# Output projection: normalized rows transposed by VectorE squares and quarter transfers instead of by TensorE

## The chip, the cores and the metric

The kernel runs on one core of a Trainium2 chip. The metric is the device time of one execution in microseconds (us); a lower time is better. The engines are named as in the profile: PE is TensorE (PEld its weight loads), DVE is VectorE, ACT is ScalarE, POOL is GpSimd, SP is SyncE, which here only issues transfers. The sixteen DMA engines move what SP, ACT and POOL issue. SBUF has 128 partitions; "quarter" below means 32 of them.

## What is computed

One decoder layer on 2048 tokens of width 1024, in float32. Two mixers (gated linear attention and dilated window attention) give `mixed`; the part around the change is the output projection, the norm behind it and the first matrix of the MLP:

```python
mixed = jnp.concatenate([o_a, o_b], axis=-1).astype(h.dtype)
h = h + jnp.einsum('bsm,md->bsd', mixed, w_out[l])

nm = rmsnorm(h, mlp_norm_g[l])
a = jnp.square(jax.nn.relu(jnp.einsum('bsd,df->bsf', nm, w_ff1[l])))
h = h + jnp.einsum('bsf,fd->bsd', a, w_ff2[l])
...
return rmsnorm(h, final_norm_g)
```

`rmsnorm(x, g)` is `x * rsqrt(mean(x*x) + 1e-6) * g` along a row.

## The kernel before

Matrix products are made from fp32r parts: each operand is split in a high part (ACT, L543) and the rest (DVE, L544), and `mm3` (L140 to L142) adds three matmuls. The big products use a scheme with seven block products in place of eight, so sums and differences of blocks are needed on both sides. The order of work on each engine comes from a planner: it places the instructions of the program by a timeline that it works out itself, and gives out the 25 slots of a shared pool of tiles (`slot`, L127) on the way; on the chip, each engine then executes its list strictly in that order and waits where an operand isn't there. A few instructions are pinned to the order of the program.

The stage of the output projection starts at L1379. Tokens lie in 16 tiles of 128 rows, taken as eight pairs (`tiles`, L1444: tile i and i+4 of a half, four pairs in each half of the tokens). Pairs 0 and 1 are made by plain products (loop at L1656), pairs 2 to 7 by the seven-product scheme (`product0`, L1634, called 42 times by the loop at L1689, with `prep0` three products ahead and four buffers `mcomb`). `load_mix` and `load_x` bring the inputs of later pairs: x of pair p+1 is issued at the third product of pair p. `mix_block` (L1465) transposes the mixer's rows on PE; the change does not touch it.

When the rows of a tile are complete, `row_done` (L1622) stores them to `hD` and queues `norm_row` for them, and after the second tile of a pair `norm_sums` too; `next_norm` (L1629) takes one of these after the first, second and sixth product of a pair, and three more in the next stage (L1871).

- `norm_row(h, t)` squares the 128x1024 rows into `scr` with a sum (ACT, L1393), makes the reciprocal root (L174, L175), scales the rows in place (DVE, L1395), transposes them on PE in eight blocks of 128x128 into two PSUM banks "c" (L1400), and copies the banks to two quarters of `bb` (ACT, L1401): `hb4[0]`, `hb4[1]` for the first tile of a pair, `hb4[2]`, `hb4[3]` for the second. `store_T` (L1385) then stores what is an operand as it stands: two blocks of the first tile, one of the second.
- `norm_sums(t, x)` makes the four sums of blocks on DVE (L1408 to L1411), one in `bb`, three in the pair's `xh` tile, and stores them.

`scr` (the second half of the tile `gs`, L1379) and `bb` are single buffers for all rows; `xh` tiles come from the shared pool and go back to it when the sums in them are stored. The stores go to `hTD` in DRAM on SP's queue. The next stage reads `hTD` in pieces (L1425), splits them (`hb`) and multiplies them with `w_ff1`, which comes through the tiles `w1raw` (L1488, POOL's queue): half 0 of the tokens, pairs 0 to 3, towards the end of this stage (`token_pieces(0, ...)`, L1688), half 1 much later.

Of the kernel before, what the change touches and what calls it, by code (L numbers as in the profile page):

```python
# [13 lines left out]
AF = mybir.ActivationFunctionType  # L14
# [4 lines left out]
D = 1024  # L19
# [95 lines left out]
def emit(tc, a, stop=99):  # L115
    nc = tc.nc
    V, A, G, T, SP = nc.vector, nc.scalar, nc.gpsimd, nc.tensor, nc.sync
# [6 lines left out]
    def ps(tag):  # L124
        return psum.tile([128, 512], F32, name="ps_" + tag, tag=tag, bufs=BANKS[tag])

    def slot(name, dt=F32, n=SLOT):  # L127

        return up.tile([128, SLOT], dt, name=name, tag="u", bufs=25)[:, :n]

    def view(t, shape):
        n = int(np.prod(shape))
        names = "abcd"[:len(shape)]
        return t[:, :n].rearrange(f"p ({' '.join(names)}) -> p {' '.join(names)}", **dict(zip(names, shape)))
# [15 lines left out]
    ident = const.tile([128, 128], F32, name="ident")  # L150
# [14 lines left out]
    def stat(n=1):  # L165
        if stat_at[0] + n > 44:
            stat_at[0] = 0
        s = stats[:, stat_at[0]:stat_at[0] + n]
        stat_at[0] += n
        return s  # L170

    def rstd_of(ssq, width, n=1, bias=eps):
        r = stat(n)
        A.activation(r, ssq, AF.Ln, bias=bias, scale=1.0 / width)  # L174
        A.activation(r, r, AF.Exp, scale=-0.5)  # L175
        return r
# [369 lines left out]
    def x_load(t, dst):  # L546
        SP.dma_start(dst, x2[t * 128:t * 128 + 128])
# [13 lines left out]
    def transposed(xt, last=None, pin=False, by=ident):  # L561
        out = []
        for q in range(2):
            pv = view(ps("cd"[q]), (4, 128))
            for k in range(4):
                of = xt[:, (4 * q + k) * 128:(4 * q + k + 1) * 128]
                ins = T.transpose(pv[:, k, :], last if last is not None and 4 * q + k == 7 else of, by)
                if pin and q + k == 0:
                    tc.keep_in_program_order(ins)
            out.append(pv)  # L570
        return out
# [33 lines left out]
    def second_half():  # L605

        b = [view(bp[:, 512 * q:], (4, 128)) for q in range(4)]
        for i in range(4):
            for k in range(2):
                x_load(8 + 4 * k + i, xp[:, D * k:D * k + D])  # L610
            yield
            for k in range(2):
                xt = xp[:, D * k:D * k + D]
                ss = stat()
                tc.keep_in_program_order(A.activation(bp[:, :D], xt, AF.Square, accum_out=ss))
                r = rstd_of(ss, D)
                V.scalar_tensor_tensor(xt, xt, r, gB, op0=OP.mult, op1=OP.mult)
            yield
            for k in range(2):
                for q, pv in enumerate(transposed(xp[:, D * k:], pin=True, by=perm)):  # L620
                    A.activation(b[2 * k + q], pv, AF.Copy)
                yield
            (b11, b21, b12, b22), (t2, t4, t3) = b, [view(xp[:, 512 * q:], (4, 128)) for q in range(3)]
            V.tensor_tensor(b12, b12, b11, op=OP.subtract)
            V.tensor_tensor(t2, b22, b12, op=OP.subtract)
            for j, v in ((2, b21), (1, b11), (5, b12), (6, t2), (3, b22), (4, t4), (7, t3)):
                if j == 5:
                    yield
                    V.tensor_tensor(t4, b21, t2, op=OP.subtract)
                    V.tensor_tensor(t3, t2, b11, op=OP.subtract)  # L630
                SP.dma_start(nTD[j - 1][:, :, i * 128:i * 128 + 128], v)
            yield

    pairs, outs = {}, {}

# [33 lines left out]
    with tc.manual_schedule(engines={nc.tensor.engine, nc.vector.engine, nc.scalar.engine, nc.gpsimd.engine}):  # L669
# [29 lines left out]
        def turned(t):  # L699
            return transposed(xs[t], by=perm)  # L700
# [6 lines left out]
        pv = turned(0)  # L707
# [9 lines left out]
        pv = turned(1)  # L717
# [6 lines left out]
        pv = turned(2)  # L724
# [6 lines left out]
        pv = turned(3)  # L731
# [17 lines left out]
        pv = turned(4)  # L749
# [5 lines left out]
        pv = turned(5)  # L755
# [4 lines left out]
        pv = turned(6)  # L760
# [4 lines left out]
        pv = turned(7)  # L765
# [60 lines left out]

    of_wo = split_wo()
    other, back, bias = second_half(), [], bias_rows()
    for at in range(7, len(jobs)):
        g = jobs[at][0]  # L830
# [512 lines left out]
    for k in range(-AHEAD, NU + LAG):  # L1343
        tr, pv, sc = iter(()), iter(()), iter(())
        if 0 <= k < NU:
            tr = units[k].transpose()
        if 0 <= k - LAG:
            u = units[k - LAG]
            u.b.v = vs[u.b.h // 2, u.b.br]
            pv = u.values()  # L1350
# [28 lines left out]
    gs, bb = slot("gs"), slot("bb")  # L1379
    gM, scr = gs[:, :D], gs[:, D:2 * D]  # L1380
    hb4 = [view(bb[:, 512 * q:], (4, 128)) for q in range(4)]
# [3 lines left out]
    def store_T(t, *which):  # L1385
        half, i = t // HT, t % 4
        for j, q in which:
            SP.dma_start(hTD[half, j - 1][:, :, i * 128:i * 128 + 128], hb4[q] if isinstance(q, int) else q)

    def norm_row(h, t):  # L1390

        ss = stat()
        A.activation(scr, h, AF.Square, accum_out=ss)  # L1393
        r = rstd_of(ss, D)
        V.scalar_tensor_tensor(h, h, r, gM, op0=OP.mult, op1=OP.mult)  # L1395
        k = t % HT // 4
        for q in range(2):
            pv = view(ps("c"), (4, 128))
            for c in range(4):
                T.transpose(pv[:, c], h[:, (4 * q + c) * 128:(4 * q + c + 1) * 128], ident)  # L1400
            A.activation(hb4[2 * k + q], pv, AF.Copy)  # L1401
        store_T(t, *(((1, 0), (2, 1)) if k == 0 else ((3, 3),)))

    def norm_sums(t, x):

        b11, b21, b12, b22 = hb4
        t2, t4, t3 = [view(v, (4, 128)) for v in (x[:, 0, :512], x[:, 0, 512:], x[:, 1, :512])]
        V.tensor_tensor(b12, b12, b11, op=OP.subtract)  # L1408
        V.tensor_tensor(t2, b22, b12, op=OP.subtract)
        V.tensor_tensor(t4, b21, t2, op=OP.subtract)  # L1410
        V.tensor_tensor(t3, t2, b11, op=OP.subtract)  # L1411
        store_T(t, (5, b12), (6, t2), (4, t4), (7, t3))
# [209 lines left out]
    def row_done(p, e):  # L1622
        t = tiles[2 * p + e]
        SP.dma_start(hD[t * 128:t * 128 + 128], xhs[p][:, e])
        norms.append((norm_row, xhs[p][:, e], t))
        if e:
            norms.append((norm_sums, t, xhs[p]))
# [28 lines left out]
    for at in range(4):  # L1656
        p, e = divmod(at, 2)
# [31 lines left out]
    for g in range(14, 56):  # L1689
        p, i = divmod(g, 7)  # L1690
# [261 lines left out]
def build(nc, inputs, stop=99):  # L1952
    arrays, aps = {}, {}
    for name in _INS:
        arrays[name] = np.ascontiguousarray(inputs[name])
    arrays.update(_constants())
    for name, v in arrays.items():
        aps[name] = nc.dram_tensor(name, v.shape, mybir.dt.from_np(v.dtype), kind="ExternalInput").ap()
    aps["out"] = nc.dram_tensor("out", (1, S, D), F32, kind="ExternalOutput").ap()
    with tile.TileContext(nc, schedule_with_timeline_sim=True) as tc:  # L1960
        emit(tc, aps, stop)
    return arrays
# [10 lines left out]
```

## Time and profile before

| | us |
|---|---|
| median of three runs | 2228.05 |
| lowest and highest of the three | 2226.95, 2230.27 |
| span of the profiled execution, first to last instruction | 2224.1 |
| the rows are normalized (first L1393 to last L1401) | about 869.5 to 1057 |
| transfers issued by SP to `hTD`, L1388 | 56 of 256 KB |

The profiled execution's time is known as its span; what lies around the span is the 4 us by which the median exceeds it. Times of instructions are counted from the span's start. A row of a timeline gives the start, the duration, engine, line, operation, output and input tiles and how many are merged. A row of a group gives the smallest, median and largest duration in ns. "SPq" is the time in which SP's sequencer issues a transfer, not the transfer itself; "to landing" is from the issue until all of its data have arrived. In a row of waits stand the total in us, the number of waits and the longest.

### The profile page before, as it was taken

Reading aid. Unit: us, or ns where it says so; the run is one execution under the profiler, and the core shown is the slowest. Engines: PE = TensorE matmul, PEld = TensorE weight load, DVE = VectorE, ACT = ScalarE, POOL = GpSimd, SP = SyncE. Lnnn points to the kernel's source line nnn. Section 1 sums busy time; section 2 is a strip of 40 time slices with the busy share of each in tenths; the row PEclk is TensorE's granted clock in tenths of the full one; section 3 lists DMA queues with packets and bytes.
Section 4 is the critical chain, followed back from the end, with each engine's and each line's share of the span. In section 5 each row is a group of like instructions: output and inputs, shape, how many; then the busy total and the mean of one; then the engine's idle time right before and its main releaser. Section 6 shows DMA issues by size and latency. Waiting matters only on the chain.

```text
span 2224.1 us, 34980 instructions
## 1 busy us (share of the span) xinstructions
PE 2205.2 (99%) x12420; PEld 1914.9 (86%) x12420; DVE 1651.5 (74%) x3092; ACT 1238.8 (56%) x2422; POOL 590.1 (27%) x625
## 2 busy tenths in 40 slices
PE   9999999999999999999999999999999999999998
PEld 8988998899999998888788888888888888888887
DVE  8676766666777877769776788777776697576788
ACT  7365424536888884547555566555555433333446
POOL 1000000035578673000000000000008543042563
PEclk9999999999999999999999999999999999999999
DMA  6566866777977976868654466555489988687775
GB/s 210 177 215 190 265 186 187 240 248 257 314 241 224 291 260 231 269 220 264 198 151 142 139 181 195 151 182 154 130 286 288 308 293 269 216 265 236 272 258 187
DMA packets 322740, 499.89 MB, mean 225 GB/s; under 512 B 20808, under 2 KB 225243, under 8 KB 311301
## 3 DMA queue, kind: packets, MB, share of 16 engines
q1 hardware_dynamic: 284434, 340.02, 47.0%
q0 software_dynamic: 30784, 104.94, 16.7%
q10 hardware_dynamic: 7346, 52.70, 6.3%
q8 instruction: 98, 1.61, 0.3%
q14 instruction: 78, 0.63, 0.1%
HBM read 339.45 MB, written 162.85 MB: 226 GB/s over the span
## 4 chain that ended last, share of the span: by engine, by line
PE 74%; issue 14%; DMA 4%; DVE 4%; ACT 2%; POOL 1%; SPq 1%; POOLq 0%; DVEq 0%; ACTq 0%
PE ps_a L142 7%; PE ps_a L141 7%; PE ps_a L140 7%; PE ps_c L142 6%; PE ps_c L141 6%; PE ps_c L140 6%; PE ps_a L1001 4%; PE ps_d L140 4%; PE ps_d L141 4%; PE ps_d L142 4%; PE ps_o L140 3%; PE ps_o L142 3%; PE ps_o L141 3%; PE ps_d L982 2%; PE ps_c L964 2%
## 5 line engine op out<-in xcount | busy, mean ns | idle before, releaser
L543 ACT ACTIVATE cb<-bs 128x1024 fp32r<-128x1024 f32 x104 | 110.3, 1060 | 286.7 <-PE ps_o L141 104.9
L544 DVE TENSOR_TENSOR cb<-bs,cb 128x1024 fp32r<-128x1024 f32 x104 | 151.7, 1459 | 129.0 <-ACT cb L543 128.5
L1488 POOL DMA_DIRECT2D w1raw<-w_ff x64 | 48.0, 750 | 701.1 <-DVE mcomb L544 504.5
L544 DVE TENSOR_TENSOR mcomb<-w1raw,mcomb 128x512 fp32r<-128x512 f32 x224 | 154.2, 689 | 93.1 <-ACT mcomb L543 93.1
L1778 POOL TENSOR_TENSOR bs<-bs,rb 128x1024 f32<-128x1024 f32 x60 | 169.4, 2824 | 201.8 <-DMA bs<-w_ff 196.5
L543 ACT ACTIVATE mcomb<-w1raw 128x512 fp32r<-128x512 f32 x224 | 140.5, 627 | 79.8 <-PE ps_c L142 26.7
L1001 PE MATMUL ps_a<-v,pt 128*128 128x65 f32 x1200 | 177.3, 253 | 1.1 <-ACT pt L989 0.7
L1001 PEld LDWEIGHTS ps_a<-v,pt 128*128 128x128 f32 x1200 | 172.7, 194 | 2.9 <-ACT pt L989 1.3
L973 ACT ACTIVATE pe<-pe,O 128x256 f32<-128x256 f32 (+1 forms) x384 | 156.2, 453 | 13.1 <-DVE O L972 10.7
L982 PE MATMUL ps_d<-ident,pe 128*128 128x128 f32 x600 | 158.6, 280 | 1.1 <-ACT pe L973 1.1
L972 DVE CUSTOM_DVE_ANT_0 pe<-ps_c,nb 128x256 f32<-128x256 f32 (+1 forms) x384 | 126.6, 360 | 39.6 <-PE ps_d L982 20.8
L304 ACT ACTIVATE wcomb<-wraw 128x512 fp32r<-128x512 f32 (+2 forms) x119 | 90.3, 759 | 111.9 <-PE ps_a L141 52.6
L544 DVE TENSOR_TENSOR ca<-ra,ca 128x1024 fp32r<-128x1024 f32 x84 | 132.6, 1579 | 0.1
L140 PE MATMUL ps_c<-hb,mcomb 128*128 128x512 f32 x320 | 124.9, 390 | 0.3 <-ACT xs L1568 0.3
L141 PE MATMUL ps_c<-hb,mcomb 128*128 128x512 f32 x320 | 124.6, 389 | 0.0
L142 PE MATMUL ps_c<-hb,mcomb 128*128 128x512 f32 x320 | 124.3, 389 | 0.0
L142 PE MATMUL ps_c<-cb,ca 128*128 128x512 f32 x312 | 121.5, 389 | 0.0
L140 PE MATMUL ps_c<-cb,ca 128*128 128x512 f32 x312 | 121.5, 389 | 0.0
L141 PE MATMUL ps_c<-cb,ca 128*128 128x512 f32 x312 | 121.5, 389 | 0.0
L982 PEld LDWEIGHTS ps_d<-ident,pe 128*128 128x128 f32 x600 | 108.3, 185 | 1.7 <-ACT pe L973 1.4
L306 DVE TENSOR_TENSOR wcomb<-wraw,wcomb 128x512 fp32r<-128x512 f32 (+2 forms) x77 | 73.3, 953 | 49.0 <-ACT wcomb L304 48.9
L1559 ACT ACTIVATE acc<-acc 128x512 f32<-128x512 f32 x96 | 60.7, 632 | 78.5 <-DVE acc L1578 36.2
(496 smaller groups left out, 7242.1 us busy)
## 6 DMA issues: line engine op xcount, KB each, us to landing
ra<-actD ACTq DMA_DIRECT2D x50, 1024.0 KB, 7.6
actD<-ring SPq DMA_DIRECT2D x176, 256.0 KB, 3.2
rb<-w_ff POOLq DMA_DIRECT2D x84, 512.0 KB, 6.2
bs<-w_ff SPq DMA_DIRECT2D x72, 512.0 KB, 5.5
w1raw<-w_ff POOLq DMA_DIRECT2D x64, 512.0 KB, 5.2
k<-kD SPq DMA_DIRECT2D x16, 1024.0 KB, 8.6
rb<-hTD SPq DMA_DIRECT2D x28, 512.0 KB, 5.7
wraw<-w_in SPq DMA_DIRECT2D x48, 256.0 KB, 3.3
```

The costliest lines, as they stand in the source:

```text
L140: T.matmul(out, sh, mh, start=first, stop=False, **kw)
L141: T.matmul(out, sl, mh, start=False, stop=False, **kw)
L142: T.matmul(out, sh, ml, start=False, stop=last, **kw)
L304: A.activation(hi, src, AF.Copy, scale=sc)
L306: V.tensor_tensor(lo, src, hi.bitcast(F32), op=OP.subtract)
L543: A.activation(hi, src, AF.Copy)
L544: V.tensor_tensor(lo, src, hi.bitcast(F32), op=OP.subtract)
L972: V.tensor_tensor_reduce(p, s, bias, scale=1.0, scalar=BIG, op0=OP.add, op1=OP.min, accum_out=nm)
L973: A.activation(p, p, AF.Exp, bias=nm, scale=-1.0)
L982: T.transpose(pb[:, i * 128:i * 128 + 128], src, ident)
L1001: T.matmul(self.b.opsum[:, n % 4], self.pt[:, i * 128:i * 128 + 128], self.b.v[:, blk, cols], start=first, stop=last)
L1778: (engines or ((G,), (V, V))[len(sums) - 1])[e].tensor_tensor(v, v, r, op=OP.add if op == "+" else OP.subtract)
```

## The change

PE's transposes and ACT's copies go. DVE transposes the scaled rows into `scr`, each square of 32x32 within itself: square (q, c, g) of source quarter q, block c and column group g stays in quarter q. `turn_blocks` then moves the squares with 16 transfers on SP's queue, one for each pair of source quarter q and destination quarter g: 32 partitions, 8 blocks, 32 elements (128 bytes) each. They go from `scr` to `bb` within SBUF. The three stores of a pair that stood in `norm_row` stand at the head of `norm_sums`.

```diff
+    def turn_blocks(dst, src):
+
+        dst = dst.rearrange("p (c t) -> p c t", t=128)
+        src = src.rearrange("p (c g t) -> p c g t", g=4, t=32)
+        for q in range(4):
+            for g in range(4):
+                SP.dma_start(dst[32 * g:32 * g + 32, :, 32 * q:32 * q + 32], src[32 * q:32 * q + 32, :, g])
...
         V.scalar_tensor_tensor(h, h, r, gM, op0=OP.mult, op1=OP.mult)
+        V.transpose(scr, h)
         k = t % HT // 4
-        for q in range(2):
-            pv = view(ps("c"), (4, 128))
-            for c in range(4):
-                T.transpose(pv[:, c], h[:, (4 * q + c) * 128:(4 * q + c + 1) * 128], ident)
-            A.activation(hb4[2 * k + q], pv, AF.Copy)
-        store_T(t, *(((1, 0), (2, 1)) if k == 0 else ((3, 3),)))
+        turn_blocks(bb[:, D * k:D * k + D], scr)
 
     def norm_sums(t, x):
 
+        store_T(t, (1, 0), (2, 1), (3, 3))
         b11, b21, b12, b22 = hb4
```

## The prediction

> **What bounds the kernel now.** I read the engine summary first, then the stretch of the changed code by windows, then the groups on the changed lines, the order of SP's queue, and at last who waited for whom.
>
> ```profile
> PE 2205.2 (99%) x12420; PEld 1914.9 (86%) x12420; DVE 1651.5 (74%) x3092; ACT 1238.8 (56%) x2422; POOL 590.1 (27%) x625
> 869.50:1056.70 187.20, 186.08 (x931) 154.63 (x930) 143.33 (x204) 104.20 (x201) 3.81 (x5) 1.00 0.78 252
> 898.40:1037.00 138.60, 137.48 (x687) 113.98 (x685) 107.89 (x156) 73.96 (x146) 3.06 (x4) 1.00 0.77 246
> ```
>
> The rows after the first are windows (length, then busy time of PE, PEld, DVE, ACT, POOL, then granted clock, DMA share, GB/s). The first is the stretch in which the 16 rows are normalized, the second is six of its eight pairs of row tiles. TensorE works 186.1 of 187.2 us at full granted clock, and DVE is at 143.3/187.2 = 77%. So this stage runs at PE's pace: 138.6/6 = 23.1 us for a pair. A microsecond taken off PE shows at the end, if nothing else becomes late; a late operand shows too.
>
> **What is removed.**
>
> ```profile
> L1400 PE MATMUL ps_c<-ident,xh x128: 270/273/301, 875.6 to 1053.1; 128*128 128x128 f32 x128
> 929.97 0.87 PE ps_c L1400 x8
> L1401 ACT ACTIVATE bb<-ps_c x32: 577/595/607, 876.5 to 1056.7; 128x512 f32<-128x512 f32 x32
> ```
>
> There are 128 transposes. One lasts 273 ns, but they are pipelined: in the chain that ended last eight of them take 0.87 us, 0.109 each. That is 128 x 0.109 = 13.9 us off PE, all on the path: the most that this change can gain. Without them a pair is 23.1 - 16 x 0.109 = 21.4 us and a row 10.7. ACT loses 32 x 0.595 = 19.0 us; it is 56% busy there (104.2/187.2), so I count this at nothing.
>
> **What is added on DVE.** 16 transposes of 128x1024, a form that the trace doesn't show. The nearest rows:
>
> ```profile
> L1395 DVE SCALAR_TENSOR_TENSOR xh<-xh,stats,gs x16: 1276/1284/1295, 872.4 to 1048.9; 128x1024 f32<-128x1024 f32 x16
> L544 DVE TENSOR_TENSOR mcomb<-ar,mcomb 128x512 fp32r<-128x512 f32 x40 | 27.2, 687 | 3.2 <-ACT mcomb L543 3.0
> L544 DVE TENSOR_TENSOR cb<-bs,cb 128x1024 fp32r<-128x1024 f32 x104 | 151.7, 1459 | 129.0 <-ACT cb L543 128.5
> ```
>
> Half the size takes 0.69 us, the same size 1.28 to 1.46. I take 1.25, near the first row, which has the same shape, one source tensor and no PSUM. Sixteen are 20 us (11 to 23) in a stretch where DVE has 187.2 - 143.3 = 43.9 idle, so the busy time is hidden by PE's matmuls. Without that cover it would cost up to 20 us. DVE would then be at 163/187 = 87%.
>
> **What is added on SP.** Each row issues 16 transfers of 32 KB (4 source quarters x 4 destination quarters, 32 partitions x 8 pieces of 128 B = 256 packets), 256 in all. They join SP's queue with all loads and stores. The nearest in the trace is a load that also has 256 packets, of 256 B (L877), and the stores of 512 packets (L1388):
>
> ```profile
> 500.44 4.74 SPq L877 DMA_DIRECT2D v<-vD  x7
> 505.40 0.41 SPq L403 DMA_DIRECT2D gvD<-acc  x1
> 505.86 4.16 SPq L877 DMA_DIRECT2D v<-vD  x6
> DMA to landing us min/median/max: 2.2/2.8/4.9
> 931.07 5.08 SPq L1388 DMA_DIRECT2D hTD<-bb  x4
> 936.23 2.21 SPq L1388 DMA_DIRECT2D hTD<-xh  x3
> 941.32 0.81 SPq L1454 DMA_DIRECT2D mx<-mixD  x2
> 942.53 0.81 SPq L1461 DMA_DIRECT2D xh<-x  x2
> 943.43 2.34 SPq L1624 DMA_DIRECT2D hD<-xh  x2
> ...
> L1388 SPq DMA_DIRECT2D hTD<-xh x24: 513/614/2647, 887.6 to 1064.5; - x24
> L1624 SPq DMA_DIRECT2D hD<-xh x16: 319/326/689, 869.5 to 1040.8; - x16
> ```
>
> Seven loads back to back hold SP for 4.74 us, six for 4.16: 0.68 to 0.69 us each, and the landing line above is theirs. Three stores take 2.21 (0.74 each), four behind a full queue 5.08 (1.27). The simplest issues, x and mix loads, are 0.81/2 = 0.41. So one quarter transfer holds SP between 0.41 and 1.27; I take 0.65, by the load with the same number of packets, less a little for a simpler pattern. A row then takes 16 x 0.65 = 10.4 us of SP, as long as PE's whole row (10.7), and its last piece lands 15 x 0.65 + 2.8 = 12.6 us after the first issue.
>
> The other issues of a pair are the five rows from 931 us on: 11.3 us as they stand, about 6.6 by the medians of the last two rows (7 x 0.61 + 0.81 + 0.81 + 2 x 0.33). With 20.8 for two rows SP has 27 to 32 us of work in a pair, against PE's 21.4.
>
> For the DMA engines a bound is the mix of 256 B and 1 KB packets at 501 to 505 us:
>
> ```profile
> q1 hardware_dynamic: 1171, 0.81, 69.7%
> ```
>
> 4 us x 16 engines x 0.697 / 1171 = 38 ns a packet. A row's 4096 packets are at most 4096 x 38/16 = 9.7 us by that, at least 2.1 us by their 512 KB at the 246 GB/s of the window. Either is below the 10.4 of issuing, so I count issue alone, but the engines are 0.77 busy already.
>
> **The new chain.** `scr` is one buffer. A row's Square (L1393) writes it, DVE's transpose writes it, the 16 transfers read it, and the next row's Square must wait until all have landed. What lies before the transfers:
>
> ```profile
> 869.55 1.06 ACT L1393 ACTIVATE gs<-xh 128x1024 f32<-128x1024 f32 x1 [5.37 <-DVE xh L1683]
> 870.51 0.18 ACT L1393 ACTIVATION_READ_ACCUMULATOR gs<-xh 128x1 f32 x1
> 870.73 0.30 ACT L174 ACTIVATE stats<-stats,pair 128x1 f32<-128x1 f32 x1
> 871.06 0.20 ACT L175 ACTIVATE stats<-stats 128x1 f32<-128x1 f32 x1
> 872.39 1.28 DVE xh L1395
> ...
> 1042.69 1.04 ACT L1393 ACTIVATE gs<-xh 128x1024 f32<-128x1024 f32 x1
> ```
>
> ACT takes 871.26 - 869.55 = 1.7 us, with the wait for the row's own store (it precedes L1395) 2.8; then 1.28 and 1.25. That is 4.2 to 5.4, I take 4.9. A row's cycle is 4.9 + 12.6 = 17.5 us (4.2 + 15 x 0.41 + 2.2 = 12.6 at the least; 5.4 + 15 x 1.27 + 2.8 = 27 at the most).
>
> From the first Square to the 16th is 173.1 us now, 15 cycles. PE's own pace would be 173.1 - 15 x 8 x 0.109 = 160.0. The chain needs 15 x 17.5 = 262.5.
>
> **What is moved.** `store_T` of a row goes from `norm_row` to the head of `norm_sums`: three stores a pair, none more than before, but on SP's queue they now stand behind both rows' transfers, and the next pair's transfers into `bb` wait for them.
>
> ```profile
> DMA to landing us min/median/max: 2.6/3.8/10.6
> ```
>
> That line is theirs (L1388): 3 x 0.61 + 3.8 = 5.6 us from the first issue. The next row's 4.9 us of Square, scaling and transpose run meanwhile; I count the 0.7 left at nothing (without that cover it would be 5.6 a pair, 45 in all). Their first readers start here, long after the stores of three of the four pairs that they need:
>
> ```profile
> 987.85 1.99 SPq L1425 DMA_DIRECT2D rb<-hTD  x4
> ```
>
> **How far the chain may lag behind PE.** ACT and DVE work in order; a Square that waits for landings holds up the splits of the next products behind it, and the sums of `norm_sums` on DVE, which wait for the second row's landings, hold up the additions that free PE's banks. Three products are prepared ahead, 3 x 21.4/7 = 9.2 us. Beyond that, rows can only lag by the tiles in the shared pool, and that is short:
>
> ```profile
> POOL w1raw L1488 <- DMA hTD<-xh: 157.1, 1, 157.1
> 1011.41 1.55 POOL L1488 DMA_DIRECT2D w1raw<-w_ff  x2 [157.14 <-DMA hTD<-xh]
> 1025.99 0.62 ACT L543 ACTIVATE mcomb<-w1raw 128x512 fp32r<-128x512 f32 x1
> DVE xh L1395 <- DMA hD<-xh: 14.5, 7, 4.2
> ```
>
> The first load of the next stage's weights starts when the sums of an earlier pair are stored, because its slot comes from that `xh`; its first use is 14.6 us later. The planner's order also puts DVE behind transfers that come later than planned: 7 of 16 rows, 14.5 us. I take a lag of one more row, 17.5, so 26.7 in all. The stall is 262.5 - (160.0 + 26.7) = 75.8 us. **Sum:** -13.9 + 75.8 = +61.9 us on the profiled 2224.1, 2286; the median of the runs shown (2228.05) lies 4.0 above that span, so **2290**. A lag between half a row and two rows gives 2299 to 2272, issues of 0.60 to 0.70 another 11 either way: 2262 to 2310 as this case's own range.
>
> **Rivals.**
> ```profile
> hD<-xh SPq DMA_DIRECT2D x16, 512.0 KB, 5.7
> ```
>
> *Faster: the transfers hide.* The decisive price is the row's cycle: up to (160.0 + 26.7)/15 = 12.4 us nothing stalls, and only the 13.9 remains: 2214. It needs 16 transfers that land together in 7.5 us. For it: a row's 512 KB as one transfer land 5.7 us after its issue (the row above), and 4.9 + 5.7 = 10.6 would do; an order that leaves the rows far behind the products would do too. Against it: the 0.68 us for each issue at 500 us.
>
> The Trainium skill, "DMA: Bandwidth & Descriptors", section "Issuing engines are not separate DMA queues", says that a sequencer's time to start a transfer is usually small beside the transfer. By it a row would cost little more than one landing and this rival would hold; the trace disagrees for small transfers, with 0.68 us of SP against a 2.8 us landing, sixteen times in a row.
>
> *Only the queue counts.* If the planner puts the Squares far enough behind, what is left is SP's work, say 29 us a pair: 8 x 29 = 232 against 187.2 now, +45. `load_x` runs six products ahead of the first use, which hides 6 x 21.4/7 = 18: +27, 2255 (2240 to 2262). For it: SP's sum alone exceeds PE's pace. Against it: one `scr`.
>
> *Everything in step.* With the 9.2 us of prepared products alone the stall is 262.5 - 169.2 = 93.3, net +79: 2307, up to 2323 with issues of 0.72.
>
> *It doesn't do what it says.* The transposes of `mix_block` in the same stage stay on PE, but the 128 of L1400 are all there is in `norm_row`. No chance of its own.
>
> **How the numbers follow.** Forecast (2262 to 2310) 0.37; faster 0.18; within 0.2%, stalls that eat just the gain, 0.06; queue only 0.20; all in step (2310 to 2335) 0.14; beyond, by a mismatch of order in the next stage, 0.05. Differences under 0.2% (4.5 us) can't be told from none by this measurement. So faster 0.18, same 0.06, slower 0.76. The range leaves out the upper 0.05 and most of the faster case: 2218 to 2335.
>
> **What would show it.** PE: no L1400, and the gain of 13.9 as less busy time. SP: 256 new issues on one line; my price is right if a run of them takes 0.6 to 0.7 us each, and the faster rival if it is below 0.35. DVE: transposes of 1.1 to 1.4. The chain: Square waits for DMA bb<-gs, several us each, 12 or more of 16 rows, and Squares 15 to 18 us apart where now 173.1/15 = 11.5. PE idle then falls on L140 behind ACT's or DVE's mcomb between 870 and 1150, and the rest of the span keeps its length. If the idle lies elsewhere, or the Squares are that far apart with PE at 99%, my lag was wrong.

## The result, and the profile after

The median after is 2356.54 us (2354.44 to 2359.84, five runs) against 2228.05 us (2223.89 to 2234.12, five runs) for the kernel before: 1.0573 times the time, 95% interval 1.0556 to 1.059. The forecast was 2290 and its range ended at 2335: the sign was right, the size too small by half. The profiled execution's span is 2354.7 us, 130.6 more than the 2224.1 of before. Wherever both are on record, the time is 1.7 to 1.9 us above the span, so the profiled execution of before took about 2226 us, 2 less than the median, and the growth by the medians is 128.5.

The page of the kernel after, with busy time and two rows of the 40 slices:

```profile
PE 2211.1 (94%) x12292; PEld 1911.0 (81%) x12292; DVE 1673.3 (71%) x3108; ACT 1225.5 (52%) x2390; POOL 589.4 (25%) x625
...
PE   9999999999999997984169999999999999999998
PEclk9999999999999998997579999999999999999999
```

TensorE has 128 instructions fewer, and yet it is 5.9 us longer busy (2205.2 before). All of TensorE's new idle time lies in the 16th to 21st of the 40 slices (59 us each), where the rows are normalized; before and behind them it is at nine tenths. The windows of the same kernel (length, busy time of PE, PEld, DVE, ACT, POOL, granted clock, DMA share, GB/s) show where in this stretch:

```profile
885.00:905.00 20.00, 12.46 (x56) 9.01 (x54) 6.24 (x8) 5.92 (x12) 0.00 (x0) 0.88 0.83 252
905.00:925.00 20.00, 12.60 (x51) 10.31 (x52) 14.64 (x23) 8.33 (x17) 0.00 (x0) 0.69 0.81 257
...
965.00:985.00 20.00, 20.00 (x95) 16.59 (x95) 15.48 (x23) 8.45 (x17) 0.00 (x0) 1.00 0.69 194
...
1085.00:1105.00 20.00, 6.57 (x16) 3.81 (x14) 6.84 (x9) 5.88 (x10) 0.65 (x1) 0.66 0.75 185
1105.00:1125.00 20.00, 0.00 (x0) 0.00 (x0) 2.53 (x2) 1.65 (x4) 0.00 (x0) 0.50 0.33 61
1125.00:1145.00 20.00, 7.55 (x22) 5.21 (x22) 9.52 (x11) 3.79 (x8) 0.75 (x1) 0.65 0.53 120
1145.00:1165.00 20.00, 0.00 (x0) 0.00 (x0) 5.04 (x6) 4.29 (x10) 0.00 (x0) 0.52 0.34 68
1165.00:1185.00 20.00, 2.07 (x4) 1.16 (x4) 5.83 (x6) 3.65 (x6) 0.00 (x0) 0.50 0.48 109
1185.00:1205.00 20.00, 5.94 (x16) 4.69 (x17) 6.62 (x11) 0.00 (x0) 0.00 (x0) 0.53 0.64 156
```

TensorE is idle for 15 of the 40 us after the first rows, nearly full in the middle, and does 22 us of work in the last 120 us. No engine is busy there: in 1105 to 1125 TensorE does nothing, VectorE 2.5 us, ScalarE 1.7. That is a chain of dependent steps. The transposes and the transfers as groups (smallest, median, largest in ns), and then SP's timeline (start, duration, how many issues) at the end of the stretch, where little else wants the queue:

```profile
L1404 DVE STREAM_TRANSPOSE gs<-xh x16: 1233/1239/1246, 875.2 to 1183.3; 128x1024 f32<-128x1024 f32 x16
```
```profile
L640 SPq DMA_DIRECT2D bb<-gs x256: 585/609/3292, 876.4 to 1195.0; - x128
...
DMA to landing us min/median/max: 1.9/2.0/9.9
```
```profile
1099.35 10.46 SPq L640 DMA_DIRECT2D bb<-gs  x16
1111.36 1.25 SPq L1396 DMA_DIRECT2D hTD<-bb  x2
1115.80 10.50 SPq L640 DMA_DIRECT2D bb<-gs  x16
```

A row's sixteen issues take 10.5 us and one transfer lands in 2.0. The Squares of the same kernel, on ScalarE's timeline (in brackets, how long the engine sat idle and for what), and the waits from 865 to 1200 us and those of TensorE (total, times, longest):

```profile
869.20 1.06 ACT L1401 ACTIVATE gs<-xh 128x1024 f32<-128x1024 f32 x1 [5.37 <-DVE xh L1688]
...
1093.46 1.06 ACT L1401 ACTIVATE gs<-xh 128x1024 f32<-128x1024 f32 x1 [1.72 <-DMA bb<-gs]
1101.22 2.00 ACT L543 ACTIVATE hb<-rb 128x1024 fp32r<-128x1024 f32 x2 [6.05 <-DMA hTD<-xh]
1111.46 1.06 ACT L1401 ACTIVATE gs<-xh 128x1024 f32<-128x1024 f32 x1 [8.24 <-DMA bb<-gs]
...
1180.28 1.06 ACT L1401 ACTIVATE gs<-xh 128x1024 f32<-128x1024 f32 x1 [8.87 <-DMA bb<-gs]
```
```profile
ACT gs L1401 <- DMA bb<-gs: 94.9, 15, 14.8
```
```profile
PE ps_c L142 <- DVE hb L544: 31.9, 1, 31.9
PE ps_a L140 <- ACT hb L543: 26.5, 1, 26.5
PE ps_a L142 <- DVE hb L544: 26.5, 1, 26.5
```

All 15 later Squares wait for landings. From the first to the 16th are 311.1 us, 138.0 more than the 173.1 of before; the span grew by 130.6. The last five cycles, with few matmuls beside them, are (1180.28 - 1093.46)/5 = 17.4 us each. How far the rows fell behind the products is seen from the additions that finish the rows, here by their group for the PSUM banks "a", which holds the last of them, in the kernel before and in the one after:

```profile
L1644 DVE TENSOR_TENSOR xh<-ps_a,xh x24: 682/686/693, 904.1 to 1040.1; 128x512 f32<-128x512 f32 x24
```
```profile
L1649 DVE TENSOR_TENSOR xh<-ps_a,xh x24: 674/684/692, 920.7 to 1054.7; 128x512 f32<-128x512 f32 x24
```

The stage's products end only 14.6 us later than before. But seven of the 16 Squares are still to come then (the 10th starts at 1069.33), and the last is 126 us behind its product; before it was 2.6 us. TensorE's large waits are for `hb`, the operand of the *next* stage. This operand is of the first half of the tokens, whose rows are long done; but its splits stand in ScalarE's and VectorE's lists between the late Squares and sums, and their slots come from `xh` tiles whose sums must be stored first (6.05 us of `hTD<-xh` in the third line of the Squares). So the rows fell far behind the products, and the stall came in the next stage, whose splits stand behind these rows.

### The profile page after: what moved, and what is told of

Its sections match the earlier page's. It is cut to its first block, busy times and chain, and to the rows that moved or that the text cites. A ratio compares the mean times of both kernels' runs of the same rounds, so it can differ in the third digit from the quotient of the medians.

```text
span 2354.7 us, 35020 instructions
## 1 busy us (share of the span) xinstructions
PE 2211.1 (94%) x12292; PEld 1911.0 (81%) x12292; DVE 1673.3 (71%) x3108; ACT 1225.5 (52%) x2390; POOL 589.4 (25%) x625
## 4 chain that ended last, share of the span: by engine, by line
PE 64%; issue 20%; DVE 5%; DMA 4%; SPq 4%; ACT 2%; POOL 1%; DVEq 0%; POOLq 0%; ACTq 0%
PE ps_a L142 6%; PE ps_a L141 6%; PE ps_a L140 6%; PE ps_c L141 6%; PE ps_c L142 6%; PE ps_c L140 6%; PE ps_a L1009 4%; SPq L640 3%; PE ps_o L140 3%; PE ps_o L141 3%; PE ps_o L142 3%; PE ps_d L140 3%; PE ps_d L141 3%; PE ps_d L142 3%; PE ps_d L990 2%
## 5 line engine op out<-in xcount | busy, mean ns | idle before, releaser
L544 DVE TENSOR_TENSOR cb<-bs,cb 128x1024 fp32r<-128x1024 f32 x104 | 159.5, 1534 | 134.6 <-ACT cb L543 134.0
L140 PE MATMUL ps_a<-hb,mcomb 128*128 128x512 f32 x232 | 91.5, 399 | 29.5 <-ACT hb L543 26.5
L142 PE MATMUL ps_a<-hb,mcomb 128*128 128x512 f32 x232 | 92.3, 398 | 26.6 <-DVE hb L544 26.5
```

The source lines that it names most:

```text
L140: T.matmul(out, sh, mh, start=first, stop=False, **kw)
L142: T.matmul(out, sh, ml, start=False, stop=last, **kw)
L544: V.tensor_tensor(lo, src, hi.bitcast(F32), op=OP.subtract)
```

## The experiments

The theory after this result: two things lengthen the stage, SP's queue, which carries 256 more issues together with every load and store of the products, and the chain of a row through the one `scr`. The rivals: VectorE (which makes the transposes and the additions that free TensorE's banks), the 128-byte pieces, the moved stores. Ratios are to the kernel before, with 95% intervals.

| run | median us | ratio | interval |
|---|---|---|---|
| e1_squares_only | 2224.62 | 0.9993 | 0.9979 to 1.0006 |
| e2_one_transfer | 2242.94 | 1.007 | 1.0052 to 1.0087 |
| e3_two_scr | 2335.91 | 1.0501 | 1.047 to 1.0532 |
| e4_half_pool | 2310.28 | 1.0374 | 1.0354 to 1.0394 |
| e5_square_apart | 2337.12 | 1.049 | 1.0471 to 1.0508 |
| e6_store_moved | 2226.93 | 0.999 | 0.9975 to 1.0006 |
| e7_act_copy | 2231.03 | 1.0011 | 1.0001 to 1.0021 |
| e8_wide_packets | 2337.26 | 1.0488 | 1.047 to 1.0506 |
| e9_transfers_beside | 2320.0 | 1.0404 | 1.0385 to 1.0423 |
| e10_two_scr_half_pool | 2289.76 | 1.0268 | 1.024 to 1.0296 |
| e11_scale_to_bb | 2218.77 | 0.9959 | 0.9944 to 0.9973 |
| e12_scale_to_scr | 2227.16 | 0.9993 | 0.9983 to 1.0003 |
| e13_through_dram | 2278.54 | 1.0219 | 1.0195 to 1.0243 |
| e14_beside_scr | 2313.71 | 1.0389 | 1.0366 to 1.0413 |
| e15_dram_seventeen | 2350.07 | 1.0554 | 1.0527 to 1.058 |

### No transfers, and one per row

```diff
-        V.transpose(scr, h)
...
-        turn_blocks(bb[:, D * k:D * k + D], scr)
+        V.transpose(bb[:, D * k:D * k + D], h)
```

> VectorE's transposes go straight into bb and the 16 quarter transfers of a row are left out, so the normalized rows reach the next stage with their squares in the wrong quarters. Theory A (the end is set by each row's cycle: scaling, transpose, 16 issues on SP, last landing, and only then the next row's Square): nothing is left to wait for, so only TensorE's 13.9 us remain: 2210 to 2218 us, ratio 0.992 to 0.996. Rival D (VectorE: 16 more instructions of 1.24 us late in front of the splits): slower than before, 2230 to 2245. Rival S (the stores moved from norm_row to norm_sums cost): 2228 or more.

```diff
-        turn_blocks(bb[:, D * k:D * k + D], scr)
+        SP.dma_start(bb[:, D * k:D * k + D], scr)
```

> One transfer of the same 512 KB per row, scr to bb within the same partitions, in place of 16: the quarter moves are left out, the wait of the next Square for scr and the waits of the sums for bb stay. Theory A says that the number of issues makes the cycle: 17.4 us becomes 4.9 + about 4 to 5.7 for one landing, 9 to 11, PE's own pace: 2210 to 2235 us. Rival B (bytes within SBUF, or any landing between the transpose and the next Square, make the loss): most of the loss stays, above 2290.

Without transfers the loss is gone, so VectorE's transposes do not cause it. But the gain of 13.9 us, which theory A expected, isn't there either; that is taken up below. With the same bytes in one transfer, within the partitions, the loss is 0.7% (some 8 us above theory A's range), and ScalarE's waits for landings, 94.9 us above, are

```profile
ACT gs L1401 <- DMA bb<-gs: 32.3, 11, 6.1
```

in the waits of that kernel from 865 to 1200 us. Moving 512 KB a row in this way is cheap; doing it in sixteen pieces, whose issues alone last 10.5 us, is not.

### The single buffer

```diff
-    gM, scr = gs[:, :D], gs[:, D:2 * D]
+    gM, two = gs[:, :D], slot("scr2")
+    scrs = [gs[:, D:2 * D], two[:, :D]]
...
+        scr = scrs[t % HT // 4]
```

> The transposed rows of a pair's first and second tile lie in two buffers (one more slot of the shared pool), so a Square waits for the transfers of the row before the last. Theory A in its narrow form (the single scr alone): the cycle is no longer serial and most of the loss goes, 2215 to 2250 us. Theory Q (SP's queue: 16 x 0.65 us for a row plus the pair's other issues, some 14 us a row against PE's 10.7): part of the loss stays, 2270 to 2320. Rival P (the planner's order and the slots, not the cycle): no change or worse, 2340 or more.

```diff
-        ss = stat()
-        A.activation(scr, h, AF.Square, accum_out=ss)
-        r = rstd_of(ss, D)
+        ss, part = stat(2), stat()
+        for n in range(2):
+            A.activation(ps("c"), h[:, 512 * n:512 * n + 512], AF.Square, accum_out=ss[:, n:n + 1])
+        A.activation(part, ss[:, 0:1], AF.Copy, bias=EPS, scale=1.0 / D)
+        r = rstd_of(ss[:, 1:2], D, bias=part)
```

> The Square's discarded output goes to two PSUM banks in halves, not to scr; the transfers stay. Only VectorE's transpose still waits for the row before to have landed, ScalarE no longer does. Theory A (one buffer in series): the cycle falls from 17.4 to 1.24 + 12.6 = about 14, and ScalarE's queue runs free; 2290 to 2335 us. Theory W (what hurts is that ScalarE's in-order queue stands 95 us): 2240 to 2280. Rival P (the planner's order and the slots decide): within 1% of the changed kernel.

A second buffer, or a Square that no longer writes `scr`, takes off 20.6 and 19.4 us of 128.5 by the medians, 16 and 18 by the ratios. Only the first opens the chain: in the second VectorE's transposes still write the one `scr`. With two buffers the last Square starts at 1139.5 and not at 1180.3, but the products end at 1087.0 and not at 1054.7. So opening the chain through `scr`, on which the prediction stood, brings little by itself. Both times lie outside the ranges of the theories for which the runs were made. The second is within 1% of the changed kernel, as its rival P said (the planner's order and the slots decide), and the first is 4 us short of its rival P: that rival is not excluded.

### The pieces, the stores, the queue

```diff
-        dst = dst.rearrange("p (c t) -> p c t", t=128)
-        src = src.rearrange("p (c g t) -> p c g t", g=4, t=32)
...
-                SP.dma_start(dst[32 * g:32 * g + 32, :, 32 * q:32 * q + 32], src[32 * q:32 * q + 32, :, g])
+                SP.dma_start(dst[32 * g:32 * g + 32, 256 * q:256 * q + 256], src[32 * q:32 * q + 32, 256 * g:256 * g + 256])
```

> Sixteen transfers a row between the same quarters and with the same 32 KB each, but every partition's 1 KB in one piece: 32 packets in place of 256 for each transfer; columns are not put where the transpose needs them. If the number of packets makes an issue cost 0.65 us: 0.41 us each as for the loads of x, the row's cycle 4.9 + 15 x 0.41 + 2 = 13, and the time falls to 2260 to 2310. If an issue costs 0.6 whatever its packets: 2335 to 2360. If the DMA engines' packets were the limit: below 2260.

```diff
-        store_T(t, *(((1, 0), (2, 1)) if k == 0 else ((3, 3),)))
...
     def norm_sums(t, x):
 
+        store_T(t, (1, 0), (2, 1), (3, 3))
```

> The kernel before with one part of the change alone: the three stores of a pair stand at the head of norm_sums and not in norm_row; TensorE transposes as before. Theories A and Q give it no price: ratio 0.998 to 1.002. If the later stores hold bb or the queue up, 1.003 or more.

Pieces of 1 KB in place of 128 B, an eighth of the packets, bring 19 us, and the issues last nearly as long as before, as the second of the three cases said. The group in the kernel with wide pieces:

```profile
L638 SPq DMA_DIRECT2D bb<-gs x256: 507/589/3117, 877.5 to 1176.7; - x128
```

The moved stores cost nothing in the kernel before. Then the transfers by themselves: the kernel before, with its transposes on TensorE, and sixteen transfers a row, pinned to the order of the program, from a constant tile to a buffer that nobody reads.

```diff
+    def beside(t):
+        dst = besD[t].rearrange("p (c t) -> p c t", t=128)
+        src = gM.rearrange("p (c g t) -> p c g t", g=4, t=32)
+        for q in range(4):
+            for g in range(4):
+                tc.keep_in_program_order(SP.dma_start(dst[32 * g:32 * g + 32, :, 32 * q:32 * q + 32], src[32 * q:32 * q + 32, :, g]))
...
+        beside(t)
```

> The kernel before, with TensorE's transposes and the old copies, and on top of it 16 transfers a row of the same shape from gM (a constant) to a place in DRAM that nobody reads: the load on SP's queue and on the DMA engines without the waits. Theory A (the wait of the next Square for the landing is what costs): little, 2228 to 2250 us. Theory Q (SP's queue: 20.8 us for two rows beside 7 to 11 of the pair's own, against PE's 23.1, so loads and stores come ever later): 2260 to 2320.

Nothing in the rows' work depends on these transfers, and they cost 92 us (2320.0 against 2227.77 for the kernel before beside it), the upper end of theory Q's range. SP's timeline in that kernel, the waits from 865 to 1250, and the group with the last addition to the rows:

```profile
979.06 10.79 SPq L1397 DMA_DIRECT2D besD<-gs  x15
989.96 1.24 SPq L1388 DMA_DIRECT2D hTD<-bb  x2
991.25 10.45 SPq L1397 DMA_DIRECT2D besD<-gs  x16
1002.10 0.55 SPq L1388 DMA_DIRECT2D hTD<-bb  x1
1002.70 1.24 SPq L1471 DMA_DIRECT2D xh<-x  x2
1004.04 0.85 SPq L1464 DMA_DIRECT2D mx<-mixD  x2
1004.99 0.44 SPq L1634 DMA_DIRECT2D hD<-xh  x1
1005.47 0.60 SPq L1388 DMA_DIRECT2D hTD<-bb  x1
1006.11 5.36 SPq L1388 DMA_DIRECT2D hTD<-xh  x3
1011.51 1.99 SPq L1471 DMA_DIRECT2D xh<-x  x1
```
```profile
DVE xh L1404 <- DMA hD<-xh: 62.8, 11, 14.8
...
PE ps_c L1410 <- DVE xh L1404: 41.2, 7, 15.3
```
```profile
L1654 DVE TENSOR_TENSOR xh<-ps_a,xh x24: 681/686/692, 910.2 to 1114.6; 128x512 f32<-128x512 f32 x24
```

From 979.06 to 1013.5, two rows (31 of their 32 transfers are shown), SP issues 33.5 of 34.4 us: the queue is full. Eight such pairs would be 275 us against the 187.2 of the stage before, 88 more, which is about the loss; this is an estimate from one pair, and the Squares' stretch itself (871.2 to 1123.2) grew by 78.9. (Three stores take 5.36 there and one load 1.99: in a full queue an issue can last longer than its own price.) The waits show one of the ways in which it reaches TensorE: the scaling in place must wait until the row has been stored to `hD`, and that store stands behind the sixteen transfers.

Here it is the products that come late: their last addition is 74.5 us later than before, where it was 14.6 in the changed kernel. So this run shows what the issues cost by themselves. It does not show that the changed kernel loses its time in the same way: there the sixteen issues are paid inside the row's cycle (10.5 of 17.4 us), behind the products.

```diff
-        V.scalar_tensor_tensor(h, h, r, gM, op0=OP.mult, op1=OP.mult)
+        V.scalar_tensor_tensor(scr, h, r, gM, op0=OP.mult, op1=OP.mult)
...
-                T.transpose(pv[:, c], h[:, (4 * q + c) * 128:(4 * q + c + 1) * 128], ident)
+                T.transpose(pv[:, c], scr[:, (4 * q + c) * 128:(4 * q + c + 1) * 128], ident)
```

> Computes the whole result, and beside it writes sixteen pieces per row to a buffer in device memory that nobody reads. It is the kernel before with the transfers beside it (ratio 1.0404), except that the scaling writes into scr, so that it does not wait for its row's store, which stands behind the transfers on SP (62.8 us of such waits). Theory S, most of the queue's price came through that wait: 2240 to 2270, ratio 1.005 to 1.02. Rival Q, the queue delays everything alike: 2300 to 2325, ratio 1.03 to 1.043, with VectorE's and TensorE's waits moved to xh<-x, mx and hb.

With that way closed 1.0389 remains of 1.0404, the intervals overlap, and the waits of this kernel from 865 to 1250 are elsewhere:

```profile
DVE xh L1654 <- DMA xh<-x: 36.3, 3, 20.5
ACT hb L543 <- DMA rb<-hTD: 34.0, 6, 14.0
```

So theory S falls and rival Q holds. In this kernel the queue delays everything that passes it; closing one way moves the wait to the next load.

### Fewer issues on SP

```diff
-                SP.dma_start(dst[32 * g:32 * g + 32, :, 32 * q:32 * q + 32], src[32 * q:32 * q + 32, :, g])
+                (SP if g < 2 else G).dma_start(dst[32 * g:32 * g + 32, :, 32 * q:32 * q + 32], src[32 * q:32 * q + 32, :, g])
```

> Eight of a row's 16 quarter transfers go by POOL's queue, which has nearly nothing else here, the other eight by SP's. Theories A and Q: issuing takes half the time if POOL's issue takes about 0.75 us like its loads of w1raw, the cycle falls from 17.4 to about 12 to 13, 2225 to 2270 us. Rival N (the DMA engines are the limit with 4096 packets of 128 bytes a row): the transfers don't land earlier, 2330 to 2360. POOL's issues could take longer with 256 packets each; then the time lies between.

The next run has this edit and the two buffers together.

> Two buffers for the transposed rows and half of the transfers on POOL's queue together; the result is whole. The buffers alone took 20 us off the changed kernel's time and the split queue 45. Theory A+Q (a cycle and a queue, each a limit by itself): together more than the sum, 2235 to 2275 us. Rival P (the planner spaces the rows by its own price of the transfers, whatever the chip does, and the next stage's tiles wait for the last rows): 2290 or more.

Half of the issues on GpSimd: 1.0374, and with two buffers 1.0268, the second best of the forms that compute the whole result. The first lies between the ranges of its theories (up to 2270, from 2330), although an issue on POOL is no longer than one on SP. The second is 15 us above the range of theory A+Q and at the edge of rival P's. The groups of the first of them, and two windows:

```profile
L640 SPq DMA_DIRECT2D bb<-gs x128: 585/616/1512, 879.6 to 1147.5; - x128
L640 POOL DMA_DIRECT2D bb<-gs x128: 582/585/637, 879.9 to 1146.3; - x128
L1401 ACT ACTIVATE gs<-xh x16: 1041/1058/1063, 872.3 to 1137.6; 128x1024 f32<-128x1024 f32 x16
```
```profile
960.00:980.00 20.00, 20.00 (x98) 16.61 (x97) 14.43 (x21) 8.32 (x16) 7.49 (x14) 1.00 0.86 214
...
1060.00:1140.00 80.00, 23.12 (x74) 16.48 (x72) 33.53 (x39) 23.84 (x45) 30.58 (x52) 0.63 0.66 149
```

A row's transfers now need 8 x 0.616 = 4.9 us of each queue, yet the Squares are still (1137.6 - 872.3)/15 = 17.7 us apart. The last five cycles are 13.1 us, as the theories expected. In the middle TensorE is full and the Squares come 15 to 33 us apart with next to no wait before them: the rows stand behind products in the lists. At the end TensorE does 23 us in 80. That the order of the lists spaces the rows is read from these windows; it wasn't tried by itself. It is what rival P says.

Last, the same move by another way: scaled into `scr`, transposed into `bb`, stored to device memory whole and loaded back in its place, by four transfers or by sixteen.

```diff
+        SP.dma_start(turnD[t], row)
+        dst = row.rearrange("p (c q t) -> p c q t", q=4, t=32)
+        src = turnD[t].rearrange("(q p) (c g t) -> g p c q t", q=4, g=4, t=32)
+        for g in range(4):
+            SP.dma_start(dst[32 * g:32 * g + 32], src[g])
...
+        V.scalar_tensor_tensor(scr, h, r, gM, op0=OP.mult, op1=OP.mult)
+        V.transpose(bb[:, D * k:D * k + D], scr)
+        turn_blocks(bb[:, D * k:D * k + D], t)
```

> Computes the whole result. The row is scaled into scr (not in place), transposed in squares straight into bb, stored to device memory with one 512 KB transfer and loaded back in its right place with four transfers of 128 KB: 5 issues per row on SP instead of 16, with the same 128-byte pieces; scr is free as soon as VectorE has read it. Queue theory: 5 x 0.6 = 3 us of SP per row, so the products keep their loads; the row's chain is Square, scaling, transpose (about 5 us), a store (about 4 us to landing) and loads (6 to 10 us), but nothing of it holds up the next row's Square. Time 2218 to 2240, ratio 0.995 to 1.005. Theory L, the length of a row's chain or the small pieces set the loss: above 2270, ratio over 1.02, with ScalarE or VectorE waiting for DMA bb.

```diff
-            SP.dma_start(dst[32 * g:32 * g + 32], src[g])
+            for q in range(4):
+                SP.dma_start(dst[32 * g:32 * g + 32, :, q], src[g][:, :, q])
```

> Computes the whole result. As the kernel that goes through device memory, but with sixteen loads of 32 KB in place of four of 128 KB: 17 issues per row on SP, 10.4 us. Queue theory: SP is full again (17 of the 12.5 us pace per row are 83 percent of it beside the other issues), 2290 to 2330, ratio 1.03 to 1.05. Theory L: within 10 us of the kernel with four loads.

Seventeen issues a row give 1.0554, five give 1.0219: 71.5 us lie between two kernels that move the same bytes in the same pieces, and differ only in how many issues it takes. Theory L, by which they were to agree within 10 us, falls there, and the queue theory falls short at the kernel with five, which was to stay below 1.005 and came out where theory L had put it; seventeen issues cost more than the queue theory's 1.05. That kernel's window of the stage, its waits from 865 to 1250, its group of loads, and one row of them on SP's timeline:

```profile
865.00:1057.00 192.00, 176.95 (x787) 142.48 (x785) 143.68 (x203) 79.85 (x150) 3.06 (x4) 0.96 0.91 265
```
```profile
DVE bb L1415 <- DMA bb<-turnD: 30.5, 6, 8.2
```
```profile
L642 SPq DMA_DIRECT2D bb<-turnD x64: 605/686/4197, 884.1 to 1120.8; - x64
```
```profile
931.14 7.69 SPq L642 DMA_DIRECT2D bb<-turnD  x4
```

The DMA engines are 0.91 busy from 865 to 1057 (0.76 in the kernel before in the same stretch), four loads are issued in 7.69 us in place of 4 x 0.686 = 2.7, and VectorE's sums wait 30.5 us for their landing. What part of the 50 us by which it is slower than the kernel before comes from the DMA engines, what from the row's longer way and what from its 80 issues stays open. It is the best form that computes the whole result, and still slower than the kernel before.

### Where the 13.9 us of TensorE went

```diff
-        V.transpose(scr, h)
...
-        turn_blocks(bb[:, D * k:D * k + D], scr)
+        A.activation(bb[:, D * k:D * k + D], h, AF.Copy)
```

> As the run with the squares alone, but ScalarE copies each scaled row into bb (about 1.06 us, in place of its two copies of 0.595) and VectorE transposes nothing: neither the transposes nor the quarter moves are done. TensorE and VectorE are then only relieved. Theory D (the run with the squares alone gained nothing because VectorE, 93% busy between 1000 and 1050 us before, is the limit of that part): the 13.9 us appear, 2211 to 2217 us, ratio 0.993 to 0.996. Rival O (the gain of 13.9 never was there, since TensorE's stage is also held by something else or the planner's new order gives it back): 2222 to 2228, ratio 0.998 to 1.001.

```diff
-        V.scalar_tensor_tensor(h, h, r, gM, op0=OP.mult, op1=OP.mult)
-        A.activation(bb[:, D * k:D * k + D], h, AF.Copy)
+        V.scalar_tensor_tensor(bb[:, D * k:D * k + D], h, r, gM, op0=OP.mult, op1=OP.mult)
```

> Leaves the transposition out altogether: VectorE's scaling writes the normalized row straight into bb (not in place into h), no ScalarE copy, no PE transposes, no transfers. It asks why the 13.9 us of TensorE work that the change takes away bring nothing (the two kernels without transposes and without transfers gave 0.9993 and 1.0011). Theory W: VectorE's list is in order, and the scaling in place waits there for the store of the row it overwrites (20.3 us of such waits in the copy kernel between 865 and 1057, 5.2 us of them right before a TensorE wait on xh); the additions that free TensorE's accumulators stand behind it. By W the waits for DMA hD<-xh vanish, TensorE loses less than 4 us between 865 and 1057, and the time is about 2214 (ratio 0.993 to 0.996). Rival R: the rest of the stage (loads of products' weights, ScalarE's order) holds the time anyway: 2225 to 2232, ratio 0.998 to 1.002, with TensorE's waits moved to other tiles.

The stretch from 865 to 1057 in the kernel before, in the one with ScalarE's copy, and in the one that scales into `bb`; behind each of the last two stands its wait of VectorE for the row's store in the same stretch:

```profile
865.00:1057.00 192.00, 190.88 (x952) 158.61 (x951) 148.13 (x211) 104.50 (x202) 3.81 (x5) 1.00 0.76 246
```
```profile
865.00:1057.00 192.00, 178.07 (x799) 145.18 (x798) 142.00 (x205) 98.57 (x179) 3.81 (x5) 0.96 0.74 235
...
DVE xh L1403 <- DMA hD<-xh: 20.3, 7, 5.6
```
```profile
865.00:1057.00 192.00, 188.29 (x863) 154.72 (x862) 156.53 (x223) 96.35 (x182) 4.85 (x7) 0.98 0.80 255
...
DVE xh L1414 <- DMA hD<-xh: 0.9, 1, 0.9
```

With the copy TensorE is idle 13.9 us of the 192, as much as it was to save, while VectorE is idle for 50: VectorE is not full, it is held. Its list is in order, and the scaling waits 20.3 us for the row's own store while the additions that free TensorE's banks stand behind it. Scaled into `bb`, that wait is 0.9, TensorE idles 3.7, and 0.9959 comes out, some 9 of the 13.9 us, as theory W had it. The copy on ScalarE is gone as well in that run, so the share of each isn't separated; the run with the squares alone has no such copy but 12.6 us of the wait, and gained nothing either. The same edit in the kernel before, where TensorE idled only 1.1 us of 192, can gain nothing:

> The kernel before, with one edit: the scaling writes into scr, and TensorE transposes from there, so that the scaling does not wait for the row's own store. By W VectorE's 14.5 us of waits for hD<-xh go; TensorE was idle for only some 4 us in this stage of the kernel before, so 0 to 4 us are gained: ratio 0.998 to 1.000. Rival: the Square of the next row, which writes scr too, now waits for TensorE's transposes, and ScalarE's list with it: 1.001 to 1.004.

Its diff is that of the kernel with transfers beside it and scaling into `scr`, made to the kernel before; 0.9993, within what can be measured.

## Why the prediction was wrong

**Right: the prices.** DVE's transpose 1.239 us (1.25 forecast); an issue 0.609 (0.65), a row of them 10.5 (10.4); the bare cycle 17.4 (17.5). The last agrees partly by luck: within a pair it is 16.4, since the first issue comes 4.3 us after the Square (4.9) and a landing takes 2.0 (2.8); to the next pair it is 17.2 to 18.8, behind the pair's sums on VectorE, which the forecast left out. `store_T` moved costs nothing. ACT's and DVE's own work is hidden. The idle time begins where "What would show it" put it, but it lasts to 1205 us and not 1150, and at the end it is on `hb`, not on `mcomb`. The faster rival falls: 0.6 us an issue. By the Trainium skill, "DMA: Bandwidth & Descriptors", section "Issuing engines are not separate DMA queues", a sequencer's time to start a transfer is usually small beside the transfer. Here it is 0.609 us against 2.0 to landing, and sixteen of them are the larger part of a row's cycle.

**Wrong: "How far the chain may lag".** The step let the chain run 26.7 us beyond PE's pace before anything stalled, 9.2 of prepared products and one row. In fact the rows lagged by seven at the end of the products, 126 us, and it saved nothing, because the splits of the next stage's `hb` stand behind these rows in the lists and take slots from their `xh`. The Squares' stretch grew by 138.0 and the span by 130.6, so 7.4 us were hidden; the forecast hid 89.4 - 61.9 = 27.5, where 89.4 is 262.5 - 173.1. That is 20 of the 69 us missed.

**Wrong: "The new chain" in the busy part.** This is the larger part of the miss. The cycle of 17.5 holds only where the row has the queue to itself. Over all 15 it was 311.1/15 = 20.7, so 48.6 us more than 262.5. Beside the products a row's sixteen issues took 10.5 to 15.6 us, and the scaling started up to 7.5 us after its Square (1.7 to 2.8 in the forecast). The prediction took the chain and SP's queue as rivals, one or the other. In the runs opening the chain brings 16 to 21 us and halving SP's issues 44, both together 68, and neither ends the loss.

**Wrong: the price of "Only the queue counts".** It was put at +27, as 29 us a pair less 18 of loads that run ahead. The transfers beside the old kernel cost 92, with 34.4 in the pair shown and no cover to be seen. Four comparisons put a price on an issue, by their ratios times 2228 us: transfers beside the old kernel, 0.0404 x 2228/256 = 0.35; half of the issues moved to GpSimd, (1.0573 - 1.0374) x 2228/128 = 0.35, and with two buffers (1.0501 - 1.0268) x 2228/128 = 0.41; seventeen against five, (1.0554 - 1.0219) x 2228/192 = 0.39. So in these kernels some 0.35 to 0.41 of each issue's 0.61 us reach the end, though not by one way: by late products in the first, in the changed kernel by the row's cycle. For 256 that is 90 to 105 of the 128.5; the one `scr` is 16 to 21. Parts measured in different kernels need not add, and the rest, 2 to 23 us, isn't traced to a cause. Three things on record could hold it: the 128-byte pieces (19 us), TensorE's longer busy time (below), and the order of the lists (rival P).

**Wrong: "What is removed" as a gain.** The 13.9 us off PE are not gained even without transfers (0.9993 and 1.0011): in these two profiled executions TensorE's busy time fell by 5.8 and 6.8 us only, and its idle time grew by 9.3 and 13.5. The prediction's own row of waits for `hD<-xh`, 14.5 us, was used for a lag only. By the run that scales into `bb`, where 9 us appear, it was the next thing late, as far as it can be told from ScalarE's copy.

## What to carry to other kernels

Add up the issuing time of a queue per stage as one does for an engine: sixteen issues a row in place of none filled a queue that shares its list with the stage's own loads, and cost 92 us though nothing needed the new transfers. Before counting an engine's saved time as a gain, look for the in-order wait that is nearly as long as the gap left: here a scaling in place that waits for the row's own store. A lag that an order of work allows is no cover if the next stage's work stands behind the rows that lag, by the order of a list or by the slots that they hold, even where it doesn't read them.

## What was not expected of the hardware

An issue of 32 KB takes nearly the same time in pieces of 128 bytes, 0.609 us, and of 1 KB, 0.589, and on GpSimd's queue, 0.585. Other transfers differ: 0.326 for a 512 KB store of rows to `hD`, 0.686 for the 128 KB loads through device memory. Between other issues some last far longer: four 7.69 us, three 5.36; what holds them isn't shown. Where TensorE stood still for most of a window of 20 us, its granted clock there was 0.50 to 0.66. After the wait that ends at 1199.06 us the next matmuls, of 128x512, start 0.43 us apart up to 1203.9, where the same form starts every 0.23 us from 1204.2 on. Over the span TensorE is busy for 2211.1 us, where 2205.2 less the 13.9 of the transposes would be 2191.3. These 20 us fit the slower restarts after the gaps, but what they add to the time wasn't measured by itself.
